# Attention scores of a hybrid encoder block: high times high as 64-row matmuls, for two query blocks in opposite halves of the array

## The chip, the cores and the metric

The kernel runs on one core of a Trainium2 chip. The metric is the device time of one execution in microseconds (us), lower is better. The engines are called as the profile calls them: PE (TensorE, the matmuls), PEld (its weight loads), DVE (VectorE), ACT (ScalarE), POOL (GpSimd), SP (SyncE, which here issues DMAs).

## What is computed

One layer of a bidirectional encoder, 1024 tokens of width 1024, all in float32. The part that matters here is the attention: two kinds, eight heads of 64 features each. Neighbourhood attention ("na") has its own keys for every head; sliding-window attention ("sw") has two key heads for eight query heads. Queries and keys are normalized by their root mean square and multiplied by gains.

```python
def rms_norm(x, g):
    xf = x.astype(jnp.float32)
    y = xf * lax.rsqrt(jnp.mean(xf * xf, axis=-1, keepdims=True) + RMS_EPS)
    return y.astype(x.dtype) * g
...
        q_a = rms_norm(q_a.reshape(B, T, NA_HEADS, HEAD_DIM), q_norm_a[l])
        k_a = rms_norm(k_a.reshape(B, T, NA_HEADS, HEAD_DIM), k_norm_a[l])
        o_a = neighbourhood_attention(q_a, k_a, v_a, rpb_a[l]).reshape(B, T, A_W)
        q_b = rms_norm(q_b.reshape(B, T, SW_HEADS, HEAD_DIM), q_norm_b[l])
        k_b = rms_norm(k_b.reshape(B, T, SW_KV_HEADS, HEAD_DIM), k_norm_b[l])
        o_b = sliding_window_attention(q_b, k_b, v_b, sink_b[l], t5_table).reshape(B, T, B_QW)
        y = (jax.nn.sigmoid(g_a) * jnp.einsum('bte,ed->btd', o_a, w_branch_a[l])
             + jax.nn.sigmoid(g_b) * jnp.einsum('bte,ed->btd', o_b, w_branch_b[l]))
        x = x + jnp.einsum('btd,de->bte', y, w_out[l])
        h = rms_norm(x, norm_ffn[l])
        u = jax.nn.silu(jnp.einsum('btd,df->btf', h, w_gate[l])) * jnp.einsum('btd,df->btf', h, w_up[l])
        x = x + jnp.einsum('btf,fd->btd', u, w_down[l])
```

Both attentions compute, for a block of queries, softmax(q k / 8 + bias) v over the keys near it.

## The kernel before

Matmuls run in a reduced float32 format ("fp32r"). To keep the precision, every operand is split in two parts: the high part is the value rounded to fp32r, the low part what is left. A product then takes three matmuls: high times high, high times low, low times high.

The tokens are permuted so that both attentions become banded: the 1024 tokens are eight blocks of 128, and a block of queries needs the keys of its own block and of the neighbours, 384 columns, or 256 for the first and the last block. The heads come in six groups (`order`, L186): four of "na" with two heads, two of "sw" with four. For every group `projection` (L236) multiplies the normalized input with the group's weights tile by tile (L325 to L327), `finish` (L329) takes the root mean squares, and `layout` (L263) transposes four tiles of queries at a time into a bank `tq` (L299) and of keys into a bank `tk` (L306).

Since a head has 64 features and the array 128 rows, a head's high and low parts share one tile. `rev_put` (L266) puts the high part of a head's queries (ACT, L277) into one half of the partitions of its tile `q`, `own`, and the low part (DVE, L278) into the other, `oth`, with the gain g multiplied in. `put_both` (L291) does the same with the keys, in a tile `k1`, and two DMAs copy it into `k2` with the halves swapped (L312, L313). The scores of a block (`scores`, L583) are then two matmuls of 128 rows into one PSUM bank: L591 with `k1` gives high times high plus low times low, L592 with `k2` the two mixed products.

The softmax follows at once: DVE adds the bias and takes the maximum (L597), ACT takes the exponential and its sum (L603), DVE the reciprocal (L604), POOL the product (L605); the result is the tile `E`, in five buffers. `flip` (L608) transposes three pieces of E on PE (L615) into a bank `tp` and splits them into `ph` (ACT, L50) and `pl` (DVE, L51); `values` (L637) multiplies these with v (L649).

The main loop (L714) goes over the 128 steps (16 heads by 8 query blocks): at step g it issues the scores of g, then the values of step g − 5, then the flip of step g − 3, and in between matmuls of the next group's projection (`fill`, L660), whose number `plan` (L712) sets. The order on PE is that of the program; the order on DVE, ACT and POOL is made by a scheduler when the kernel is built. There are two PSUM banks for scores (`s`), two for `tp`, three for projections and `tq`, `tk`, one for the output. After the attention, branch products, output projection and feed-forward (a seven-product scheme, L824 to L826) run until the end.

A table for the "sw" bias is made once near the start by a matmul with 32 rows and 8 columns (`window_table`, L542).

Of the kernel before, what the change touches and what calls it, by code (L numbers as in the profile page):

```python
# [19 lines left out]
HD = 64  # L20
# [5 lines left out]
def block_kernel(ctx, tc, x, xt, small, w_in, rpb, t5, w_ba, w_bb, w_out, w_gate, w_up, w_down,  # L26
# [18 lines left out]
    def f(ap):  # L45
        return ap.bitcast(F32)
# [55 lines left out]
    def tok(t):  # L102
        return slice(t * P, (t + 1) * P)
# [60 lines left out]
    def load_small():  # L164
        nc.scalar.dma_start(cols, small)
        nc.vector.tensor_scalar_mul(nsink, nsink, -1.0)
        for b in "ab":
            nc.vector.tensor_scalar_mul(gk[b], gk[b], HD ** 0.5)

    warm = cst.tile([P, 1], F32, name="warm")  # L170
    nc.scalar.activation(warm, mhalf[:, 0:1], AF.Exp)
# [64 lines left out]
    def projection(gi, weights, pending, after=None):  # L236
# [17 lines left out]
        def both(parts):  # L254

            if gi:
                for part in parts:
                    part()()
            else:
                for low in [part() for part in parts]:  # L260
                    low()

        def layout(s0):  # L263
            sw = kind == "sw"

            def rev_put(z, own, oth, src, g):  # L266

                if sw:
                    def to(z, rows):
                        return z[rows, :].rearrange("p (b r h x) -> p b r h x", b=8, r=2, h=2)[:, :, :, 1 - s0 // 4, :]  # L270
                    src = src.rearrange("p (b r x) -> p b r x", b=8, r=2)[:, :, ::-1, ::-1]
                else:
                    def to(z, rows):
                        return z[rows, s0 * P:(s0 + 4) * P].rearrange("p (b x) -> p b x", b=4)
                    src = src.rearrange("p (b x) -> p b x", b=4)[:, :, ::-1]
                hi_of, lo_of = to(z, own), to(z, oth)
                nc.scalar.activation(hi_of, src, AF.Copy, scale=g)  # L277
                return lambda: nc.vector.scalar_tensor_tensor(lo_of, src, g, f(hi_of), op0=ALU.mult, op1=ALU.subtract)  # L278

            def spot(tp, rows, j):  # L280
                return tp[rows, :].rearrange("p (r s c) -> p s r c", s=4, r=16)[:, j] if sw else tp[rows, tok(j)]

            def rows16(z):
                return z.rearrange("p (r x) -> p r x", r=16) if sw else z

            def put(z, rows):
                if not sw:
                    return z[rows, s0 * P:(s0 + 4) * P]
                return z[rows, :].rearrange("p (r h x) -> p r h x", r=16, h=2)[:, :, s0 // 4, :]

            def put_both(z, own, oth, src, g):  # L291
                nc.scalar.activation(put(z, own), rows16(src), AF.Copy, scale=g)
                return lambda: nc.vector.scalar_tensor_tensor(put(z, oth), rows16(src), g, f(put(z, own)),
                                                              op0=ALU.mult, op1=ALU.subtract)

            def pair(p_):
                tq = bank("pj" if gi or not s0 else "t", f"tq{gi}_{s0}_{p_}")
                for j in range(4):
                    nc.tensor.transpose(spot(tq, slice(0, P), j), qns[s0 + j][:, tok(p_)], ident)  # L299
                both([lambda e=e, own=own, oth=oth: rev_put(q[2 * p_ + e], own, oth, tq[own, :], gq[b][own, :])  # L300
                      for e, (own, oth) in enumerate(SIDES)])

            def keys():
                tk = bank("pj" if gi else "o", f"tk{gi}_{s0}")
                for j in range(4):
                    nc.tensor.transpose(spot(tk, slice(0, nk * HD), j), qns[s0 + j][:, nq * HD:nqk], ident)  # L306
                both([lambda e=e, own=own, oth=oth: put_both(k1[e], own, oth, tk[own, :], gk[b][own, :])
                      for e, (own, oth) in enumerate(SIDES[:nk])])
                for e, (own, oth) in enumerate(SIDES[:nk]):
                    for c in ([slice(0, T)] if s0 and kind == "sw" else  # L310
                              [slice(s0 * P, s0 * P + 512)] if kind == "na" else []):
                        nc.sync.dma_start(f(k2[e][oth, c]), f(k1[e][own, c]))  # L312
                        nc.sync.dma_start(f(k2[e][own, c]), f(k1[e][oth, c]))  # L313

            def done():
                if s0 == 4:
                    if late_v:
                        split(v[0][:, :, 0, :], v[0][:, :, 1, :], late_v.pop())
                    ready.add(gi)

            return [keys] + [lambda p_=p_: pair(p_) for p_ in range(nq // 2)] + [done]
# [7 lines left out]
        def finish(tiles):  # L329
# [2 lines left out]
            ss = ap.tile([P, 16], F32, tag="ss", name=f"ss{gi}_{t0}", bufs=4)[:, :n * nh]  # L332
            norms = ss.rearrange("p (t h) -> p t h", h=nh)
            for i, (t, ps) in enumerate(tiles):
                qn = ap.tile([P, 320], F32, tag="qn", name=f"qn{gi}_{t}", bufs=7)
                nc.scalar.activation(qn[:, :nqk], ps[:, :nqk], AF.Square)
                nc.vector.tensor_reduce(norms[:, i], qn[:, :nqk].rearrange("p (h e) -> p h e", e=HD),
                                        axis=AX.X, op=ALU.add)
                qns.append(qn)
# [189 lines left out]
    with tc.tile_pool(name="at", bufs=1) as ap:  # L529
# [50 lines left out]
            heads += [dict(gi=gi, kind=kind, hl=hl, kl=hl * nk // nq, h=idx * nq + hl, nq=nq, O={}, E={}, P={})  # L580
                      for hl in range(nq)]

        def scores(hd, qb):  # L583
            q, k1, k2, v = groups[hd["gi"]]
            nm_ = f"{hd['gi']}_{hd['hl']}_{qb}"
            b0, b1 = max(0, qb - 1), min(7, qb + 1)
            n = (b1 - b0 + 1) * P
            s = bank("s", "s" + nm_)
            qs = q[hd["hl"]][:, tok(qb)]
            ks = slice(b0 * P, b0 * P + n)  # L590
            nc.tensor.matmul(s[:, :n], qs, k1[hd["kl"]][:, ks], start=True, stop=False)  # L591
            nc.tensor.matmul(s[:, :n], qs, k2[hd["kl"]][:, ks], start=False, stop=True)  # L592
            E = ap.tile([P, 388], F32, tag="E", name="E" + nm_, bufs=5)
            nm = ap.tile([P, 2], F32, tag="nm", name="nm" + nm_, bufs=5)
            sw = hd["kind"] == "sw"
            sk = nsink[:, hd["h"]:hd["h"] + 1]
            att["bound"] = nc.vector.tensor_tensor_reduce(E[:, :n], s[:, :n], hd["bias"](qb), -1.0, sk if sw else 1e30,  # L597
                                           ALU.add, ALU.min, nm[:, 0:1]).ins
            m = n
            if sw:  # L600
                nc.gpsimd.tensor_copy(E[:, n:n + 1], sk)
                m = n + 1
            nc.scalar.activation(E[:, :m], E[:, :m], AF.Exp, bias=nm[:, 0:1], scale=-1.0, accum_out=nm[:, 1:2])  # L603
            nc.vector.reciprocal(nm[:, 1:2], nm[:, 1:2])  # L604
            nc.gpsimd.tensor_scalar(E[:, :n], E[:, :n], nm[:, 1:2], 1.0, op0=ALU.mult, op1=ALU.mult)  # L605
            hd["E"][qb] = E

# [106 lines left out]
        for g in range(n + LP):  # L714
            before = plan[g - 1] if g else due[0]
            if g < n:
# [2 lines left out]
                    fill(done_chunks[1] + 1)  # L719
                if g == 0:  # L720
                    opening.close()
                scores(hd, qb)
                if qb == 1 and g + 8 < n:
                    load_bias(steps[g + 8][0])
                if qb == (4 if g + 16 >= n else 6) and g + 8 - qb < n:
# [794 lines left out]
```

## Time and profile before

| what | value |
|---|---|
| median of 3 runs | 1317.51 us (1315.83 to 1317.52) |
| span of the profiled execution | 1314.8 us (no other time is given for it) |
| granted clock | 1.000 |
| busy in 54 to 120 us | PE 65.42, DVE 49.57, ACT 45.31, POOL 37.30 of 66 us |
| busy in 340 to 380 us | PE 38.74, DVE 30.76, ACT 26.18, POOL 13.43 of 40 us |
| busy in 400 to 700 us | PE 299.15, DVE 242.96, ACT 145.32 of 300 us |

The profile is of one execution. Busy times are unions of an engine's instructions; matmuls are pipelined, and their recorded durations overlap, so the distance between two starts says more of a matmul's price than its duration. A row of the timeline has the start, the time, the engine, the line, the operation, output and inputs, the shape, how many rows are merged, and in brackets the idle time before it with what ended it. "issue" there is a wait for nothing that the profile shows. For a matmul "128*128 128x384" is the loaded part (rows times columns) and what streams through it.

### The profile page before, as it was taken

The page shows a single profiled execution, that of the slowest core. Times are in us where ns is not written, and L with a number is a line of the kernel's source. Part 1 is how long each engine was busy: PE and PEld are TensorE (multiplying, and loading weights), DVE is VectorE, ACT ScalarE, POOL GpSimd, SP SyncE. Part 2 cuts the span into 40 slices and gives each one's busy share as a digit, 9 for nine tenths or more (in the row PEclk, how much of TensorE's full clock was granted, in tenths as well). Part 3 has the DMA queues.
Part 4 walks back from the last instruction along what each step waited for, and adds up shares of the span by engine and source line. Part 5 has one row for each costly group of instructions (what it writes and reads, how often), then busy time and mean ns, then how long its engine had stood idle before and what let it go on. Part 6 is the DMA issues. An engine that isn't in the chain of part 4 may idle for free.

```text
span 1314.8 us, 19624 instructions
## 1 busy us (share of the span) xinstructions
PE 1304.5 (99%) x6618; PEld 1133.6 (86%) x6618; DVE 1018.5 (77%) x2039; ACT 695.8 (53%) x1459; POOL 182.5 (14%) x322
## 2 busy tenths in 40 slices
PE   9999999999999999999999999999999999999998
PEld 8999999999888788888888888888888888888887
DVE  5678867776687758868999878888777799798774
ACT  6677857776664324636456544443444455363532
POOL 1364645564310000000000000000000000000000
PEclk9999999999999999999999999999999999999999
DMA  9532424252435348757774533233233356672532
GB/s 306 153 89 61 108 64 109 61 135 61 143 118 180 121 146 271 240 172 237 241 247 120 169 105 106 87 104 117 81 108 121 120 171 217 245 248 65 183 129 81
DMA packets 180997, 191.92 MB, mean 146 GB/s; under 512 B 21104, under 2 KB 126576, under 8 KB 180896
## 3 DMA queue, kind: packets, MB, share of 16 engines
q1 hardware_dynamic: 180640, 190.57, 46.5%
q8 instruction: 52, 0.85, 0.3%
q14 instruction: 49, 0.40, 0.1%
q10 hardware_dynamic: 256, 0.10, 0.0%
HBM read 133.19 MB, written 52.37 MB: 141 GB/s over the span
## 4 chain that ended last, share of the span: by engine, by line
PE 85%; DVE 6%; DMA 4%; ACT 2%; issue 1%; SPq 1%; POOL 1%; ACTq 0%; POOLq 0%; DVEq 0%
PE bankZ L824 6%; PE bankZ L825 5%; PE bankZ L826 5%; PE bankY L824 5%; PE bankY L826 5%; PE bankY L825 5%; PE pj L327 4%; PE bankX L824 4%; PE pj L326 4%; PE pj L325 4%; PE bankX L825 4%; PE bankX L826 4%; PE o L649 3%; PE bankV L825 3%; PE bankV L824 3%; PE bankV L826 3%
## 5 line engine op out<-in xcount | busy, mean ns | idle before, releaser
L603 ACT ACTIVATE E<-E,nm 128x384 f32<-128x384 f32 (+3 forms) x128 | 75.7, 592 | 48.3 <-DVE nm L597 42.4
L605 POOL TENSOR_SCALAR E<-E,nm 128x384 f32<-128x384 f32 (+1 forms) x128 | 74.3, 581 | 95.2 <-DVE nm L604 72.3
L51 DVE TENSOR_TENSOR pl<-tp,ph 128x384 fp32r<-128x384 f32 (+1 forms) x128 | 66.4, 519 | 17.2 <-ACT ph L50 16.2
L50 ACT CAST ph<-tp 128x384 fp32r<-128x384 f32 (+1 forms) x128 | 57.4, 449 | 20.5 <-PE tp L615 19.9
L50 ACT CAST f<-f 128x512 fp32r<-128x512 f32 x87 | 50.9, 620 | 22.2 <-DMA f<-u_dram 21.5
L51 DVE TENSOR_TENSOR f<-f 128x512 fp32r<-128x512 f32 x87 | 56.4, 684 | 8.0 <-ACT f L50 8.0
L615 PE MATMUL tp<-ident,E 128*128 128x128 f32 x352 | 59.5, 272 | 0.9 <-POOL E L605 0.9
L615 PEld LDWEIGHTS tp<-ident,E 128*128 128x128 f32 x352 | 45.2, 140 | 5.9 <-POOL E L605 1.2
L345 POOL TENSOR_TENSOR ss<-ss,mhalf 128x4 f32<-128x4 f32 (+2 forms) x42 | 49.7, 1184 | 3.2
L649 PE MATMUL o<-pl,v 128*128 128x256 f32 (+2 forms) x160 | 48.7, 305 | 0.6 <-DVE pl L51 0.5
L604 DVE RECIPROCAL nm<-nm 128x1 f32<-128x1 f32 x128 | 20.4, 160 | 36.1 <-ACT E L603 34.8
L1214 POOL TENSOR_TENSOR rs<-rs,mhalf 128x4 f32<-128x4 f32 x2 | 2.8, 1418 | 319.4 <-DVE rs L1213 319.4
L649 PE MATMUL o<-ph,v 128*128 128x256 f32 (+2 forms) x160 | 45.9, 301 | 0.5 <-ACT ph L50 0.5
L591 PE MATMUL s<-k,q 128*128 128x384 f32 (+1 forms) x128 | 46.0, 359 | 0.0
L592 PE MATMUL s<-k,q 128*128 128x384 f32 (+1 forms) x128 | 41.4, 323 | 0.0
L597 DVE CUSTOM_DVE_ANT_0 E<-s,bsw,cols 128x384 f32<-128x384 f32 (+1 forms) x64 | 37.0, 577 | 4.5 <-PE s L592 3.8
L1231 ACT ACTIVATE u<-u 128x512 f32<-128x512 f32 x44 | 27.5, 629 | 19.7 <-DVE u L1230 19.7
L597 DVE CUSTOM_DVE_ANT_0 E<-s,bna 128x384 f32<-128x384 f32 (+1 forms) x64 | 32.9, 517 | 4.2 <-PE s L592 3.7
L1232 DVE TENSOR_TENSOR u<-u,wide_rs 128x512 f32<-128x512 f32 x44 | 30.0, 687 | 6.4 <-ACT u L1231 5.6
L50 ACT CAST f_5h<-s1f 128x512 fp32r<-128x512 f32 x22 | 13.7, 622 | 39.5 <-DVE s1f L806 32.2
L824 PE MATMUL bankY<-f,f_6h 128*128 128x512 f32 x88 | 34.5, 392 | 0.1
L825 PE MATMUL bankV<-f,f_5h 128*128 128x512 f32 x88 | 34.4, 391 | 0.0
(1268 smaller groups left out, 4658.9 us busy)
## 6 DMA issues: line engine op xcount, KB each, us to landing
f<-u_dram SPq DMA_DIRECT2D x77, 256.0 KB
wg_s<-in_w_gate_dram SPq DMA_DIRECT2D x22, 512.0 KB
u_dram<-u SPq DMA_DIRECT2D x33, 256.0 KB
o_dram<-of SPq DMA_DIRECT2D x32, 256.0 KB
o<-o_dram SPq DMA_DIRECT2D x32, 256.0 KB
sg<-g_dram SPq DMA_DIRECT2D x32, 256.0 KB
g_dram<-go SPq DMA_DIRECT2D x24, 256.0 KB
u_dram<-tau SPq DMA_DIRECT2D x22, 256.0 KB
```

The source lines that it names most:

```text
L50: a = nc.scalar.copy(hi, src)
L51: b = (eng or nc.vector).tensor_tensor(lo, src, f(hi), ALU.subtract)
L325: nc.tensor.matmul(ps[:, :384], lh, his[k][:, :384], start=(k == 0), stop=False)
L326: nc.tensor.matmul(ps[:, :384], lh, los[k][:, :384], start=False, stop=False)
L597: att["bound"] = nc.vector.tensor_tensor_reduce(E[:, :n], s[:, :n], hd["bias"](qb), -1.0, sk if sw else 1e30, ALU.add, ALU.min, nm[:, 0:1] ...
L603: nc.scalar.activation(E[:, :m], E[:, :m], AF.Exp, bias=nm[:, 0:1], scale=-1.0, accum_out=nm[:, 1:2])
L605: nc.gpsimd.tensor_scalar(E[:, :n], E[:, :n], nm[:, 1:2], 1.0, op0=ALU.mult, op1=ALU.mult)
L615: nc.tensor.transpose(tp[:, tok(j)], hd["E"][qq][:, ko:ko + P], ident)
L649: nc.tensor.matmul(hd["O"][half][:, (a - half * 4) * P:(z + 1 - half * 4) * P], v[:, kb].rearrange("p a e -> p (a e)"), pp[:, (a - q0) * P ...
L824: nc.tensor.matmul(ps, hi[:, tok(j)], bh, start=first, stop=False, skip_group_check=True)
L825: nc.tensor.matmul(ps, hi[:, tok(j)], bl, start=False, stop=False, skip_group_check=True)
L826: nc.tensor.matmul(ps, lo[:, tok(j)], bh, start=False, stop=end, skip_group_check=True)
```

## The change

Each pair of query blocks (2i, 2i + 1) of a head is now scored together, on every even step. For each of the two blocks one full matmul of 128 rows gives the two mixed products; then a matmul of 64 rows gives high times high alone, for one block in the lower half of the array and for the other in the upper half (`tile_position`). For the second block's high part to lie in the other half, `rev_put` now swaps the halves for every second block, so it puts each half in two pieces. The product of the two low parts is no longer added. The queries' gain is multiplied into the keys' gain at the start. Buffers of E go from five to six, of `qn` from seven to six.

```diff
         for b in "ab":
-            nc.vector.tensor_scalar_mul(gk[b], gk[b], HD ** 0.5)
+            nc.vector.scalar_tensor_tensor(gk[b], gk[b], HD ** 0.5, gq[b], op0=ALU.mult, op1=ALU.mult)
...
-            def rev_put(z, own, oth, src, g):
+            def rev_put(z, own, oth, src):
...
-                hi_of, lo_of = to(z, own), to(z, oth)
-                nc.scalar.activation(hi_of, src, AF.Copy, scale=g)
-                return lambda: nc.vector.scalar_tensor_tensor(lo_of, src, g, f(hi_of), op0=ALU.mult, op1=ALU.subtract)
+                def part(par):
+                    own_, oth_ = (oth, own) if par else (own, oth)
+                    hi_of, lo_of = (to(z, rows)[:, par::2] for rows in (own_, oth_))
+                    nc.scalar.copy(hi_of, src[:, par::2])
+                    return lambda: nc.vector.tensor_tensor(lo_of, src[:, par::2], f(hi_of), ALU.subtract)
+
+                lows = [part(par) for par in range(2)]
+                return lambda: [low() for low in lows]
...
-                both([lambda e=e, own=own, oth=oth: rev_put(q[2 * p_ + e], own, oth, tq[own, :], gq[b][own, :])
+                both([lambda e=e, own=own, oth=oth: rev_put(q[2 * p_ + e], own, oth, tq[own, :])
...
-                qn = ap.tile([P, 320], F32, tag="qn", name=f"qn{gi}_{t}", bufs=7)
+                qn = ap.tile([P, 320], F32, tag="qn", name=f"qn{gi}_{t}", bufs=6)
...
-        def scores(hd, qb):
+        def scores(hd, qa):
+
             q, k1, k2, v = groups[hd["gi"]]
+            z, kl = q[hd["hl"]], hd["kl"]
+            high = [k1[kl], k2[kl]] if kl == 0 else [k2[kl], k1[kl]]
+            made = []
+            for par in range(2):
+                qb, e = qa + par, (hd["hl"] + par) % 2
+                b0, b1 = max(0, qb - 1), min(7, qb + 1)
+                n, ks = (b1 - b0 + 1) * P, slice(b0 * P, (b1 + 1) * P)
+                s = bank("s", f"s{hd['gi']}_{hd['hl']}_{qb}")
+                made.append((qb, e, s, n, ks))
+                nc.tensor.matmul(s[:, :n], z[:, tok(qb)], high[1 - e][:, ks], start=True, stop=False)
+            for qb, e, s, n, ks in made:
+                rows = slice(e * HD, (e + 1) * HD)
+                nc.tensor.matmul(s[:, :n], z[rows, tok(qb)], high[e][rows, ks], start=False, stop=True,
+                                 tile_position=(e * HD, 0))
+            for qb, e, s, n, ks in made:
+                softmax(hd, qb, s, n)
+
+        def softmax(hd, qb, s, n):
+
             nm_ = f"{hd['gi']}_{hd['hl']}_{qb}"
-            b0, b1 = max(0, qb - 1), min(7, qb + 1)
-            n = (b1 - b0 + 1) * P
-            s = bank("s", "s" + nm_)
-            qs = q[hd["hl"]][:, tok(qb)]
-            ks = slice(b0 * P, b0 * P + n)
-            nc.tensor.matmul(s[:, :n], qs, k1[hd["kl"]][:, ks], start=True, stop=False)
-            nc.tensor.matmul(s[:, :n], qs, k2[hd["kl"]][:, ks], start=False, stop=True)
-            E = ap.tile([P, 388], F32, tag="E", name="E" + nm_, bufs=5)
-            nm = ap.tile([P, 2], F32, tag="nm", name="nm" + nm_, bufs=5)
+            E = ap.tile([P, 388], F32, tag="E", name="E" + nm_, bufs=6)
+            nm = ap.tile([P, 2], F32, tag="nm", name="nm" + nm_, bufs=6)
...
-                scores(hd, qb)
+                if not qb % 2:
+                    scores(hd, qb)
```

In the changed kernel the full score matmuls are L600 and the 64-row ones L603; the first operation of the softmax is L615 there, the transposes of `flip` L633, the values L667, the projections L330 to L332.

On PE, in the second group's last head, the rows around block 2 before the change. The names are the output and then the inputs: `s_3_2` is the score bank of head 3 of the group, block 2, `tp` the flipped bank, `pj` the projection's:

```order
L615 MATMUL tp_2_6_2291<-ident,E_2_6_2161 128x128
L615 MATMUL tp_2_6_2291<-ident,E_2_7_2198 128x128
L591 MATMUL s_3_2_2299<-k_0_655,q_3_653 128x384
L592 MATMUL s_3_2_2299<-k_0_656,q_3_653 128x384
L325 MATMUL pj_0_2227<-wg_5h,h_0_94 128x384
L326 MATMUL pj_0_2227<-wg_5l,h_0_94 128x384
L327 MATMUL pj_0_2227<-wg_5h,h_0_94 128x384
```

Block 3 follows eighteen rows after block 2, behind the next flip:

```order
L615 MATMUL tp_2_7_2335<-ident,E_2_6_2161 128x128
L615 MATMUL tp_2_7_2335<-ident,E_2_7_2198 128x128
L591 MATMUL s_3_3_2342<-k_0_655,q_3_653 128x384
L592 MATMUL s_3_3_2342<-k_0_656,q_3_653 128x384
L325 MATMUL pj_0_2227<-wg_7h,h_0_95 128x384
```

The same place of PE after the change:

```order
L633 MATMUL tp_2_6_2319<-ident,E_2_6_2192 128x128
L633 MATMUL tp_2_6_2319<-ident,E_2_7_2199 128x128
L600 MATMUL s_3_2_2327<-k_0_659,q_3_657 128x384
L600 MATMUL s_3_3_2329<-k_0_660,q_3_657 128x384
L603 MATMUL s_3_2_2327<-k_0_660,q_3_657 128x384
L603 MATMUL s_3_3_2329<-k_0_659,q_3_657 128x384
L330 MATMUL pj_0_2255<-wg_5h,h_0_94 128x384
L331 MATMUL pj_0_2255<-wg_5l,h_0_94 128x384
L332 MATMUL pj_0_2255<-wg_5h,h_0_94 128x384
```

The two score matmuls of block 3 have moved up beside those of block 2, into one run of four, of which the two L603 have 64 rows.

On DVE, the same two blocks before (`E` is the softmax tile, `pl` the low part of a flipped one, `nm` the maximum and the sum; the L597 row named ISA is the bias and the maximum):

```order
L597 ISA E_3_2_2302,nm_3_2_2303<-s_3_2_2299,bsw_1989,cols 128x384
L597 ISA nm_3_2_2303 128x1
L51 TENSOR_TENSOR pl_2_6_2296<-tp_2_6_2291,ph_2_6_2295 128x384
L604 RECIPROCAL nm_3_2_2303<-nm_3_2_2303 128x1
L597 ISA E_3_3_2345,nm_3_3_2346<-s_3_3_2342,bsw_1989,cols 128x384
L597 ISA nm_3_3_2346 128x1
L293 SCALAR_TENSOR_TENSOR k_0_1197<-tk_4_2322,cols,k_0_1197 64x512
```

And after the change:

```order
L615 ISA E_3_2_2333,nm_3_2_2334<-s_3_2_2327,bsw_2017,cols 128x384
L615 ISA nm_3_2_2334 128x1
L51 TENSOR_TENSOR pl_2_6_2324<-tp_2_6_2319,ph_2_6_2323 128x384
L615 ISA E_3_3_2340,nm_3_3_2341<-s_3_3_2329,bsw_2017,cols 128x384
L615 ISA nm_3_3_2341 128x1
L622 RECIPROCAL nm_3_2_2334<-nm_3_2_2334 128x1
L622 RECIPROCAL nm_3_3_2341<-nm_3_3_2341 128x1
L298 SCALAR_TENSOR_TENSOR k_0_1213<-tk_4_2360,cols,k_0_1213 64x512
```

The second block's bias and maximum stand ahead of the first block's reciprocal now, and both reciprocals follow together.

On DVE again, where the queries of the second group are laid out, before (`tq` is the bank of transposed queries, `q` the tile of a head):

```order
L278 SCALAR_TENSOR_TENSOR q_0_650<-tq_0_0_931,cols,q_0_650 64x16x32
L51 TENSOR_TENSOR pl_0_1_948<-tp_0_1_943,ph_0_1_947 128x384
L597 ISA E_0_5_957,nm_0_5_958<-s_0_5_954,bna_294 128x384
L597 ISA nm_0_5_958 128x1
L278 SCALAR_TENSOR_TENSOR q_1_651<-tq_0_0_931,cols,q_1_651 64x16x32
```

And after:

```order
L622 RECIPROCAL nm_0_5_937<-nm_0_5_937 128x1
L280 TENSOR_TENSOR q_0_654<-tq_0_0_948,q_0_654 64x4x2x32 x2
L51 TENSOR_TENSOR pl_0_1_969<-tp_0_1_964,ph_0_1_968 128x384
L280 TENSOR_TENSOR q_1_655<-tq_0_0_948,q_1_655 64x4x2x32 x2
L342 TENSOR_REDUCE ss_5_981<-qn_5_982 128x5
```

Each put of a query's low part is two instructions ("x2") of half the columns in place of one.

## The prediction

> **What bounds the kernel now.** I read the page first (busy shares, then the chain that ended last), then the waits of TensorE in the attention stage, the busy times by stretch, and last the timeline around single matmuls.
>
> ```profile
> span 1314.8 us, 19624 instructions
> ...
> PE 1304.5 (99%) x6618; PEld 1133.6 (86%) x6618; DVE 1018.5 (77%) x2039; ACT 695.8 (53%) x1459; POOL 182.5 (14%) x322
> ...
> PE 85%; DVE 6%; DMA 4%; ACT 2%; issue 1%; SPq 1%; POOL 1%; ACTq 0%; POOLq 0%; DVEq 0%
> ```
>
> PE is busy for 99% of the span and carries 85% of the chain. The score matmuls, which the change touches, stand in one stage:
>
> ```profile
> L591 PE MATMUL s<-k,q x128: 278/341/423, 55.7 to 380.0; 128*128 128x384 f32 x96, 128*128 128x256 f32 x32
> ```
>
> So 128 score tiles (96 of 384 columns, 32 of 256) are made between 55.7 and 380.0 us, one every 2.55 us. In that stage PE waits for other engines only this long (engine, line, releaser: total us, times, longest):
>
> ```profile
> PE tp L615 <- POOL E L605: 0.9, 1, 0.9
> PE tq L299 <- DVE k L293: 0.6, 1, 0.6
> PE o L649 <- DVE pl L51: 0.5, 2, 0.3
> PE o L649 <- ACT ph L50: 0.5, 1, 0.5
> PE tk L306 <- DVE qn L366: 0.5, 1, 0.5
> PE pj L326 <- DVE wg_6l L51: 0.2, 1, 0.2
> ```
>
> That is 3.2 us in all, of 324. A PE time added or saved there moves the end one for one, except for what these 3.2 us can take up. The other engines have room; the next row has a stretch, its length, the busy time (and instructions) of PE, PEld, DVE, ACT and POOL, then the granted clock and the DMA:
>
> ```profile
> 212.00:265.00 53.00, 52.90 (x350) 51.67 (x349) 41.81 (x135) 39.95 (x110) 25.75 (x58) 1.00 0.31 80
> ```
>
> DVE, the fullest of them, has 41.81 of 53 us, 79%.
>
> **The price of a matmul.** A matmul's duration in the records overlaps the next one's, so I go by the distance between starts.
>
> ```profile
> 302.25 0.34 PE L327 MATMUL pj<-wg_7h,h 128*128 128x384 f32 x1
> 302.43 0.33 PE L591 MATMUL s<-k,q 128*128 128x384 f32 x1
> 302.60 0.33 PE L592 MATMUL s<-k,q 128*128 128x384 f32 x1
> 302.78 0.33 PE L325 MATMUL pj<-wg_0h,h 128*128 128x384 f32 x1
> ...
> 306.84 0.28 PE L649 MATMUL o<-ph,v 128*128 128x256 f32 x1
> 306.96 0.28 PE L649 MATMUL o<-pl,v 128*128 128x256 f32 x1
> 307.08 0.34 PE L325 MATMUL pj<-wg_6h,h 128*128 128x384 f32 x1
> ...
> 307.62 0.60 PE L306 MATMUL tk<-ident,qn 128*128 128x128 f32 x4
> 308.05 0.49 PE L615 MATMUL tp<-ident,E 128*128 128x128 f32 x3
> ```
>
> 384 columns take 0.175 us (0.35 for the two from 302.43 to 302.78), 256 columns 0.12, and 128 columns in plain float32 0.108 (four in 0.43, so 512 such columns 0.43). The weight loads hide behind the matmul before.
>
> **What changes on PE.** Per pair of query blocks there were four full matmuls, two to a block; now there are two full ones and two of 64 rows, in the lower and the upper half. If the halves ran wholly side by side and nothing else cost anything, one matmul of 0.175 would go per inner pair. But the program now goes from 128 rows to 64 and back in each of 64 pairs, and the trace has one place where the row shape changes: the table product L542, of 32 rows and 8 columns, between full matmuls. First PE, then its weight loads:
>
> ```profile
> 24.29 0.33 PE L326 MATMUL pj<-wg_7l,h 128*128 128x384 f32 x1
> 24.46 0.34 PE L327 MATMUL pj<-wg_7h,h 128*128 128x384 f32 x1
> 24.73 1.02 PE L542 MATMUL pswe<-oh,t5s 32*8 32x512 f32 x2
> 25.68 0.44 PE L325 MATMUL pj<-wg_0h,h 128*128 128x384 f32 x1
> 25.96 0.33 PE L326 MATMUL pj<-wg_0l,h 128*128 128x384 f32 x1
> ```
>
> ```profile
> 24.29 0.19 PEld L327 LDWEIGHTS pj<-wg_7h,h 128*128 128x128 f32 x1
> 24.73 0.09 PEld L542 LDWEIGHTS pswe<-oh,t5s 32*8 32x8 f32 x2 [0.25 <-issue]
> 25.68 0.19 PEld L325 LDWEIGHTS pj<-wg_0h,h 128*128 128x128 f32 x1 [0.86 <-ACT rows L150]
> 25.79 0.19 PEld L326 LDWEIGHTS pj<-wg_0l,h 128*128 128x128 f32 x1
> ```
>
> Everywhere else a load starts with the matmul before it (24.29 and 24.29). Here the load of L542 does not start at 24.46 but at 24.73, and "issue" says that it waited for nothing the profile shows. **Going in** costs 0.27 − 0.175 = 0.095. **Coming out**: two passes of 0.43 from 24.73 end at 25.59, and the next load starts at 25.68, 0.09 later; that load then lies bare, since the matmul behind it starts 0.28 after it, not 0.175, which is 0.105 more. The row names ACT's L150 as releaser; what L325 takes from ACT there is a part of h, written before the rows of x are squared, so I take the gap for the shape's. Going in, the load of L542 has only 8 columns; a score's has 128, so I add a bare load of 0.105 there too. Two changes of shape: 0.095 + 0.105 + 0.09 + 0.105 = 0.395 us per pair.
>
> The second half needs a load as well. The nearest row has the next load 0.11 after a bare one (25.68, 25.79), so I start the second half 0.11 after the first; side by side with it, this is 0 (both loads at once), one behind the other 0.175. Then:
> - two inner pairs per head (384 and 384): the halves took 2 × 0.175 = 0.35; now 0.395 + 0.11 + 0.175 = 0.68; +0.33 each.
> - first pair (256, 384): 0.295 before; 0.68 now; +0.385.
> - last pair (384, 256): 0.295 before; 0.395 + 0.11 + 0.12 = 0.625 now; +0.33.
> Per head 0.33 × 3 + 0.385 = 1.375, for 16 heads **+22.0 us**. With both loads at once it is 0.22 × 2 + 0.275 × 2 = 0.99, +15.8; with the halves one behind the other 4 × 0.395, +25.3. I take the row's 0.11 and keep both ends.
>
> A change of columns alone shows no such price:
>
> ```profile
> 92.28 0.33 PE L327 MATMUL pj<-wg_6h,h 128*128 128x384 f32 x1
> 92.46 0.60 PE L306 MATMUL tk<-ident,qn 128*64 128x128 f32 x4
> ```
>
> The transposes with 64 columns follow at the usual 0.18. The Trainium skill, "TensorEngine Tiling (Array Packing)", section Key Properties, says that changing the tiling mode drains the TensorE, and makes no difference between rows and columns. The row shape at 24.73 agrees with its 0.095, the column shape at 92.46 does not; by the rule the sum stays at +22.0, without it it would be the first rival's.
>
> **What else changes.** The queries' parts are now put in two pieces each: 32 puts become 64, on ACT and on DVE.
>
> ```profile
> L277 ACT ACTIVATE q<-tq,cols x32: 667/685/688, 39.4 to 344.1; 64x512 fp32r<-64x512 f32 x32
> ...
> L278 DVE SCALAR_TENSOR_TENSOR q<-tq,cols,q x32: 744/750/758, 40.8 to 344.8; 64x512 fp32r<-64x512 f32 x32
> ...
> L50 ACT CAST ph<-tp 128x256 fp32r<-128x256 f32 x31 | 11.4, 368 | 8.7 <-PE tp L615 8.3
> ...
> L51 DVE TENSOR_TENSOR pl<-tp,ph 128x256 fp32r<-128x256 f32 x31 | 13.0, 419 | 5.4 <-ACT ph L50 4.8
> ```
>
> A piece of 256 columns costs 0.368 on ACT and 0.419 on DVE by the nearest rows, so 32 × (0.736 − 0.685) = 1.6 us more of ACT and 32 × (0.838 − 0.750) = 2.8 us of DVE. PE's own work hides them; uncovered they cost up to 4.4. The gains that leave L277 and L278 go into the key gain, one instruction in place of one at the start: nothing. The softmaxes now come two at a time:
>
> ```profile
> L603 ACT ACTIVATE E<-E,nm 128x384 f32<-128x384 f32 (+3 forms) x128 | 75.7, 592 | 48.3 <-DVE nm L597 42.4
> L605 POOL TENSOR_SCALAR E<-E,nm 128x384 f32<-128x384 f32 (+1 forms) x128 | 74.3, 581 | 95.2 <-DVE nm L604 72.3
> ...
> L604 DVE RECIPROCAL nm<-nm 128x1 f32<-128x1 f32 x128 | 20.4, 160 | 36.1 <-ACT E L603 34.8
> ...
> L597 DVE CUSTOM_DVE_ANT_0 E<-s,bsw,cols 128x384 f32<-128x384 f32 (+1 forms) x64 | 37.0, 577 | 4.5 <-PE s L592 3.8
> ```
>
> One takes 0.577 + 0.592 + 0.16 + 0.581 = 1.9 us, the second some 0.6 more; the flip that needs it stands two steps on, 5.1 us, so PE's other work covers it. Behind the second L597 on DVE stand both reciprocals, then the next flip's low part, which the values need two steps later: covered too. If that cover were gone in the few places where PE waits already, those 3.2 us might double; the odd block's E being made a step earlier may take away the 0.9 behind POOL's E. Six E buffers where there were five keep the distance to reuse; one qn buffer less could show as a longer wait of tq or tk (0.6 and 0.5 now). I take 0 for all of this, with −1 to +4.
>
> Against it, PE falls behind by 1.375 us per head, and each present wait is under 1 us, so the other engines catch up: I take off all 3.2 us (ends 0 and 3.2).
>
> **Sum.** 22.0 − 3.2 = +18.8 us on a span of 1314.8: 1333.6. No separate time is given for the profiled execution; its span lies 2.7 under the median of the three timed runs, 1317.5, so the forecast is 1317.5 + 18.8 = **1336.3 us**, 1.4% slower.
>
> **Rivals.**
> - *No price for the shape* (the one that ends faster): loads stay hidden, the halves overlap. Inner pair 0.175 + 0.11 against 0.35, −0.065; first −0.01; last −0.065: −0.205 per head, −3.3 us, 1314.2. With both loads at once −0.175 and −0.12, twice each: −9.4 us, 1308.1. For it: the 64-column transposes, and that L542 is one place, of another size. Against: nothing else explains 24.73. It decides if the two changes together cost under 0.065 to 0.175 us per pair.
> - *Both loads at once*: the halves start together, +15.8 − 3.2 = +12.6, 1330.1. The Trainium skill, "TensorE: Matmul & The Clock Gate", section "Part 3: Packing small matmuls — row/col tiling", has matmuls of different row groups start about 4 ns apart, and loads overlap running matmuls only where the row group differs; no row here shows two row groups at work. For it: the two loads of L542 stand within 0.09 us; against: these have 8 columns.
> - *Halves not side by side*: the change then does not do what it says. With the price +25.3 − 3.2 = +22.1, 1339.6; without it no change, 1317.5.
> - *Only one way costs* (say coming out): 0.1975 per pair, the halves overlapping: 0.1325 × 3 + 0.1875 per head, +9.4, less half of the 3.2: +7.8, 1325.3.
>
> **How the numbers follow.** Forecast 0.38, both loads at once 0.20, one behind the other with the price 0.08, one way only 0.06: slower 0.72. No price with overlap 0.17, half of it at −9.4 and half at −3.3; no change at all 0.11. A measurement of this kernel tells about 0.2%, 2.6 us, from no change; part of the −3.3 falls inside that, so faster 0.14, same 0.14. The likeliest case's own range, with the side terms, is 1329 to 1343. The 8-in-10 range leaves out the no-price cases (0.17) and little else: **1316 to 1343**.
>
> **What would show it.** In the changed trace: the load of the first half (L603) starts with its matmul some 0.27 after the second full one (L600) rather than beside it, and the next full matmul's load starts about 0.09 after the halves' end with the following matmul 0.28 on; from the first full matmul of a pair to the one after it I expect about 1.03 us, where it was 0.70. Only L600 and L603 and their neighbours should be farther apart; after 400 us everything should be shifted, not longer. I am wrong if the loads of L603 start beside the matmuls ahead of them, or if the waits behind DVE and POOL grow past 5 us.

## The result and the profile after

| | before | after |
|---|---|---|
| median, range | 1317.51 us (1315.83 to 1317.78, 4 runs) | 1336.51 us (1335.52 to 1337.96, 4 runs) |
| profiled execution, span | 1314.8 us | 1335.4 us (its time 1337.23) |

The ratio is 1.0153, with an interval of 1.0139 to 1.0167: 19.0 us slower, where 18.8 were forecast. The total was right, but by luck: terms of it were wrong, and their errors cancelled. The three lines of the page that answer to those of before:

```profile
span 1335.4 us, 19668 instructions
...
PE 1321.6 (99%) x6618; PEld 1124.0 (84%) x6618; DVE 1024.9 (77%) x2071; ACT 695.3 (52%) x1491; POOL 182.1 (14%) x322
...
PE 86%; DVE 4%; DMA 4%; POOL 2%; ACT 1%; issue 1%; SPq 1%; ACTq 0%; POOLq 0%; DVEq 0%
```

PE is still the bound, with as many matmuls as before. The end of the program is only shifted. One matmul of the feed-forward, from the view of its tile, first in the kernel before, then in the one after (first and last start at the end):

```profile
L826 PE MATMUL bankV<-f,f_5l x88: 389/389/389, 686.7 to 1073.4; 128*128 128x512 f32 x88
```

```profile
L845 PE MATMUL bankV<-f,f_5l x88: 389/389/389, 707.5 to 1093.9; 128*128 128x512 f32 x88
```

It starts 20.8 us later at its first instance and 20.5 later at its last, so all of the time came ahead of it. One inner pair of the kernel after, from the timeline, PE and then its weight loads (two rows merged are "x2", the time then runs from the first start to the last end):

```profile
227.24 0.51 PE L600 MATMUL s<-k,q 128*128 128x384 f32 x2
227.69 0.44 PE L603 MATMUL s<-k,q 64*128 64x384 f32 x2
228.06 0.44 PE L330 MATMUL pj<-wg_2h,h 128*128 128x384 f32 x1
228.34 0.34 PE L331 MATMUL pj<-wg_2l,h 128*128 128x384 f32 x1
```

```profile
227.08 0.36 PEld L600 LDWEIGHTS s<-k,q 128*128 128x128 f32 x2
227.69 0.19 PEld L603 LDWEIGHTS s<-k,q 64*128 64x128 f32 x2 [0.25 <-issue]
228.06 0.19 PEld L330 LDWEIGHTS pj<-wg_2h,h 128*128 128x128 f32 x1 [0.19 <-issue]
```

From the first full matmul to the halves 0.45 us, from the halves to the next full matmul 0.37, from that to its successor 0.28: 1.10 us, where five full matmuls in a row need 5 × 0.175 = 0.875. That is +0.225 for this pair. The load of the halves waits for "issue", as L542's did, and it does so in all 64 pairs, 14.4 us together. The two loads of L603 together last 0.19, as long as one, and its two matmuls 0.44, as long as a single matmul behind a bare load (L330 at 228.06): the halves start together. For a pair of 384 and 256 columns:

```profile
204.26 0.47 PE L600 MATMUL s<-k,q 128*128 128x384 f32 x2
204.65 0.44 PE L603 MATMUL s<-k,q 64*128 64x384 f32 x2
205.02 0.44 PE L330 MATMUL pj<-wg_7h,h 128*128 128x384 f32 x1
205.30 0.34 PE L331 MATMUL pj<-wg_7l,h 128*128 128x384 f32 x1
```

This is 1.04 us against 2 × (0.175 + 0.12) + 0.175 = 0.765, +0.275. With two pairs of each kind per head that is 16 × 2 × (0.22 + 0.275), the prediction's +15.8 us for both loads at once. What PE waited for in the attention stage (50 to 410 us; total us, times, longest):

```profile
PE o L667 <- DVE pl L51: 3.3, 5, 0.9
PE o L667 <- ACT ph L50: 1.3, 2, 0.8
PE tk L311 <- DVE nm L622: 0.5, 1, 0.5
PE tq L304 <- DVE k L298: 0.4, 1, 0.4
PE tq L304 <- DVE q L280: 0.2, 1, 0.2
```

These waits were 3.2 us before and are 5.7 now; the new ones are in front of `values`, for `ph` and `pl`. Just after the worst of them the clock falls. Two stretches, with the busy times of PE, PEld, DVE, ACT and POOL, then the granted clock:

```profile
157.00:166.00 9.00, 7.15 (x43) 6.20 (x43) 5.55 (x19) 5.91 (x18) 5.85 (x11) 0.99 0.66 189
166.00:169.50 3.50, 3.50 (x13) 2.75 (x12) 1.70 (x6) 1.82 (x5) 0.92 (x3) 0.53 0.23 62
```

After 9 us in which PE was idle for 1.85, the clock was 0.53 for 3.5 us, which costs about 3.5 × 0.47 = 1.6 us. The Trainium skill, "TensorE: Matmul & The Clock Gate", section "What's actually happening", has the clock halve after an idle window of some 3.4 us; the halving agrees, but no single wait of PE in the list above is longer than 0.9 us. What sets the halving off is not shown: the 9 us from 287 us on have 1.70 us of idle PE, and the 3.5 us behind them a clock of 1.00; and of the four executions one had a mean clock of 1.000 (1335.52 us).

### The profile page after: what moved, and what is told of

It reads as the page before. It is cut to its first block, busy times and chain, and to the rows that moved or that the text cites. A ratio compares the mean times of both kernels' runs of the same rounds, so it can differ in the third digit from the quotient of the medians.

```text
span 1335.4 us, 19668 instructions
## 1 busy us (share of the span) xinstructions
PE 1321.6 (99%) x6618; PEld 1124.0 (84%) x6618; DVE 1024.9 (77%) x2071; ACT 695.3 (52%) x1491; POOL 182.1 (14%) x322
## 4 chain that ended last, share of the span: by engine, by line
PE 86%; DVE 4%; DMA 4%; POOL 2%; ACT 1%; issue 1%; SPq 1%; ACTq 0%; POOLq 0%; DVEq 0%
PE bankZ L843 6%; PE bankZ L844 6%; PE bankZ L845 6%; PE bankY L844 5%; PE bankY L843 5%; PE bankY L845 5%; PE pj L330 5%; PE bankX L843 4%; PE bankX L845 4%; PE bankX L844 4%; PE pj L332 4%; PE pj L331 4%; PE o L667 3%; PE bankV L844 3%; PE bankV L843 3%; PE bankV L845 3%
## 5 line engine op out<-in xcount | busy, mean ns | idle before, releaser
L633 PE MATMUL tp<-ident,E 128*128 128x128 f32 x352 | 59.3, 272 | 0.0
L667 PE MATMUL o<-pl,v 128*128 128x256 f32 (+2 forms) x160 | 49.2, 308 | 3.3 <-DVE pl L51 3.3
L633 PEld LDWEIGHTS tp<-ident,E 128*128 128x128 f32 x352 | 45.1, 140 | 4.7
L667 PE MATMUL o<-ph,v 128*128 128x256 f32 (+2 forms) x160 | 46.8, 306 | 1.3 <-ACT ph L50 1.3
L615 DVE CUSTOM_DVE_ANT_0 E<-s,bsw,cols 128x384 f32<-128x384 f32 (+1 forms) x64 | 35.3, 580 | 9.4 <-PE s L603 7.6
L615 DVE CUSTOM_DVE_ANT_0 E<-s,bna 128x384 f32<-128x384 f32 (+1 forms) x64 | 31.2, 521 | 9.0 <-PE s L603 7.3
L667 PEld LDWEIGHTS o<-pl,v 128*128 128x128 f32 x160 | 30.6, 191 | 5.4 <-DVE pl L51 4.4
L843 PE MATMUL bankZ<-f,f_4h 128*128 128x512 f32 x88 | 34.5, 392 | 0.4 <-DVE p L1367 0.4
L844 PE MATMUL bankV<-f,f_5h 128*128 128x512 f32 x88 | 34.4, 391 | 0.0
L843 PE MATMUL bankV<-f,f_5h 128*128 128x512 f32 x88 | 34.4, 391 | 0.0
L844 PE MATMUL bankZ<-f,f_4h 128*128 128x512 f32 x88 | 34.4, 390 | 0.0
```

The costliest lines, as they stand in the source:

```text
L633: nc.tensor.transpose(tp[:, tok(j)], hd["E"][qq][:, ko:ko + P], ident)
L667: nc.tensor.matmul(hd["O"][half][:, (a - half * 4) * P:(z + 1 - half * 4) * P], v[:, kb].rearrange("p a e -> p (a e)"), pp[:, (a - q0) * P ...
L843: nc.tensor.matmul(ps, hi[:, tok(j)], bh, start=first, stop=False, skip_group_check=True)
L844: nc.tensor.matmul(ps, hi[:, tok(j)], bl, start=False, stop=False, skip_group_check=True)
```

## The experiments

The theory after the first look: the price of the row shape is that of both loads at once, +15.8 us, and pairing the scores adds waits. The rivals: the halves don't overlap, the two-piece puts cost something, or the pairing costs nothing and the shape all.

**Pairing with full rows.** L603 again with all 128 rows, which adds the product of the low parts; all else as after.

```diff
-                rows = slice(e * HD, (e + 1) * HD)
-                nc.tensor.matmul(s[:, :n], z[rows, tok(qb)], high[e][rows, ks], start=False, stop=True,
-                                 tile_position=(e * HD, 0))
+                nc.tensor.matmul(s[:, :n], z[:, tok(qb)], high[e][:, ks], start=False, stop=True)
```

> The changed kernel with the second two matmuls of a pair at 128 rows again (which adds the product of the low parts back); pairing, swapped halves, two-piece puts and buffers stay. Shape theory: the changes of row shape cost 0.22 us a pair as the starts in the changed trace show, 15.8 us in all, so 1336.5 - 15.8 = 1320.7 us, 1319 to 1323. Rival, pairing: the time comes from softmaxes two at a time and from the puts, and it stays above 1330.

Measured 1327.60 us (1322.55 to 1329.13), ratio 1.0071 (1.0048 to 1.0094). A miss for both theories: without any change of shape the pairing already costs about 10 us. Much of that goes with the clock: the one of the four executions whose mean clock was 1.000 took 1322.55 us, 5.4 over the median of the kernel before at 1.000 in the same runs (1317.15), and the other three (0.997 to 0.999) 1326.53 and more. In the profiled execution, at 0.999, in 50 to 410 us PE waits 3.7 us for `pl`, 1.6 for `ph`, 1.6 for a transfer of the keys and 2.3 for smaller ones, 9.2 in all, and the clock falls here too:

```profile
163.00:165.00 2.00, 2.00 (x9) 2.00 (x8) 1.13 (x4) 0.89 (x2) 0.45 (x2) 0.51 0.44 120
165.00:168.00 3.00, 3.00 (x19) 2.96 (x18) 0.74 (x4) 1.42 (x5) 0.85 (x3) 0.76 0.03 5
```

**A half alone.** The kernel before, block by block, with its second score matmul over 64 rows; the product of the low parts is left out.

```diff
-            nc.tensor.matmul(s[:, :n], qs, k1[hd["kl"]][:, ks], start=True, stop=False)
-            nc.tensor.matmul(s[:, :n], qs, k2[hd["kl"]][:, ks], start=False, stop=True)
+            nc.tensor.matmul(s[:, :n], qs, high[1 - e][:, ks], start=True, stop=False)
+            nc.tensor.matmul(s[:, :n], z[rows, tok(qb)], high[e][rows, ks], start=False, stop=True,
+                             tile_position=(e * HD, 0))
```

> The kernel before, unpaired, with the mixed products at 128 rows and high times high at 64 rows, one half alone per block (the product of the low parts is left out). Shape theory: 128 blocks pay going in and coming out with nothing side by side, 0.39 us each, +50 us: 1367, 1362 to 1372. Rival, the pair's 0.37 us from the first half to the next full matmul is two loads one behind the other and no wait after the halves: 0.29 each, +37 us: 1354.

Measured 1362.06 us (1360.54 to 1363.80), ratio 1.0340 (1.0324 to 1.0355): the price comes with every change of shape, so twice as often. One block and then the waits of PE in 50 to 410 us:

```profile
209.57 0.34 PE L594 MATMUL s<-k,q 128*128 128x384 f32 x1
209.84 0.44 PE L595 MATMUL s<-k,q 64*128 64x384 f32 x1
210.21 0.44 PE L325 MATMUL pj<-wg_3h,h 128*128 128x384 f32 x1
```

```profile
PE tq L299 <- DVE k L293: 0.2, 1, 0.2
```

Going in takes 0.27 and from the half to the next full matmul 0.37, the same 0.37 as with two halves: the second half is free. Of 3.2 us of waits 0.2 are left, so here PE's delay did take them up. 128 × 0.395 − 3.0 is +47.6; the span grew by 46.4, of which 44.3 stand ahead of the feed-forward (its first bankV starts at 731.0, before at 686.7) and about 1.7 are a stretch from 745.2 to 748.6 us at a clock of 0.51. So the sum is some 3 us high; that was not attributed.

**Both in one half.** The kernel after with both blocks in the same half of the array.

```diff
-                    own_, oth_ = (oth, own) if par else (own, oth)
+                    own_, oth_ = own, oth
...
-                qb, e = qa + par, (hd["hl"] + par) % 2
+                qb, e = qa + par, hd["hl"] % 2
```

> The changed kernel with both blocks' high parts in the same half of the array, no swap. If the halves run side by side in the changed kernel, this loses it: 0.175 for two inner pairs and 0.12 for two outer pairs of a head, 9.4 us on top of 1336.5: 1346, more (1351) if the second half's load lies bare too. Rival, they do not overlap now: 1336.5 as it is.

Measured 1344.01 us (1341.77 to 1345.83), ratio 1.0197 (1.0179 to 1.0214), 7.5 us over the kernel after. The pair that stood at 227.24:

```profile
228.84 0.51 PE L600 MATMUL s<-k,q 128*128 128x384 f32 x2
229.28 0.61 PE L603 MATMUL s<-k,q 64*128 64x384 f32 x2
229.83 0.45 PE L330 MATMUL pj<-wg_2h,h 128*128 128x384 f32 x1
```

The halves now take 0.55 instead of 0.37: one streams after the other. So in the kernel after they do lie side by side. The loss of 7.5 is less than the 9.4 expected; this trace has no stretch of half clock (1.6 us in the kernel after).

**The two-piece puts alone.** The kernel before with each half put in two pieces (not swapped), the gain in the keys and six `qn` buffers.

> The kernel before with the queries put in two pieces (not swapped), the gain moved to the keys and six qn buffers; scores as before. Shape theory: hidden, 1317.5 within 2.6. Rival, puts: some 4 us slower, 1321.

Measured 1316.46 us (1314.70 to 1319.14, 10 runs), ratio 0.9994 (0.9985 to 1.0003): no difference, as taken in the prediction.

**What pairing waits for.** The waits of the kernel after for `ph` and `pl` lead to the weights of the next group, whose last two pieces are split into parts (`wg_6h`, `wg_7h` on ACT, `wg_6l` on DVE) from a staging tile `wg_3s`. ACT, then PE, then DVE in the kernel after:

```profile
162.11 0.51 ACT L50 CAST wg_6h<-wg_3s 128x384 fp32r<-128x384 f32 x1 [2.42 <-DMA wg_3s<-in_w_in_dram]
162.53 0.51 ACT L50 CAST wg_7h<-wg_3s 128x384 fp32r<-128x384 f32 x1
162.94 0.47 ACT L50 CAST ph<-tp 128x384 fp32r<-128x384 f32 x1
```

```profile
162.35 0.34 PE L332 MATMUL pj<-wg_3h,h 128*128 128x384 f32 x1
163.47 0.33 PE L667 MATMUL o<-ph,v 128*128 128x128 f32 x1 [0.77 <-ACT ph L50]
164.68 0.33 PE L667 MATMUL o<-pl,v 128*128 128x128 f32 x1 [0.89 <-DVE pl L51]
```

```profile
162.66 0.56 DVE L51 TENSOR_TENSOR wg_6l<-wg_3s,wg_6h 128x384 fp32r<-128x384 f32 x1 [2.36 <-ACT wg_6h L50]
163.13 0.48 DVE L615 CUSTOM_DVE_ANT_0 E<-s,bsw,cols 128x256 f32<-128x256 f32 x1
...
163.53 0.61 DVE L615 CUSTOM_DVE_ANT_0 E<-s,bsw,cols 128x384 f32<-128x384 f32 x1
...
164.07 0.55 DVE L51 TENSOR_TENSOR pl<-tp,ph 128x384 fp32r<-128x384 f32 x1
```

A wait in brackets counts from the recorded end of the matmul before it. L332 and L667 start 1.12 us apart where 0.175 is usual, so the listed 0.77 costs 0.95: a wait behind such a matmul costs some 0.17 us more than the lists say. ACT stands for 2.42 us behind a transfer, with `ph` behind it on the same engine; DVE stands behind ACT and then works through two score blocks before `pl`. The same splits on ACT in the kernel before:

```profile
154.31 0.49 ACT L50 CAST ph<-tp 128x384 fp32r<-128x384 f32 x1
154.78 0.51 ACT L50 CAST wg_6h<-wg_3s 128x384 fp32r<-128x384 f32 x1
...
275.09 0.51 ACT L50 CAST wg_6h<-wg_3s 128x384 fp32r<-128x384 f32 x1 [0.52 <-DMA wg_3s<-in_w_in_dram]
...
275.92 0.47 ACT L50 CAST ph<-tp 128x384 fp32r<-128x384 f32 x1
```

There one `ph` stood ahead of the split, and the other behind it, for a transfer that was 0.52 us late; in the kernel after both stand behind it, and both transfers are some 2.4 us late. The view of the tile `wg_3s` sums such waits of ACT, before and then after:

```profile
  DMA wg_3s<-in_w_in_dram: 0.7, 2
```

```profile
  DMA wg_3s<-in_w_in_dram: 5.2, 3
```

The theory became: the pairing's cost is this split ahead of `ph`. The rival: it is the two softmaxes that now come at once. Four runs, with the two splits issued later, in the first tile of the next group's projection:

```diff
-                if after and t == 7 and k:
+                if gi > 1 and t == 0 and k in (1, 3):
+                    weights.split(6 + k // 2)
+                if after and t == 7 and 0 < k < 7:
                     after.split(k - 1)
...
-            if after and t == 7:
-                after.split(7)
```

on the kernel after,

> The changed kernel with the splits of the last two weight tiles of a group (which on ACT wait for the transfer of wg_3s, with a flip's ph queued behind them) moved behind the start of the next group. If the time beside the shape's 15.8 us comes from there, the stalls near 163 and 293 us of the changed trace go, with the half clock that follows the first: some 6 us, 1330.5, 1329 to 1333. If it comes from elsewhere: 1336.5.

on the pairing with full rows,

> The paired kernel with full rows (e1_full_rows) and the same late splits. Wait theory: from 1327.6 to 1321, 1319 to 1323. Rival, two softmaxes at a time: 1327.6 stays.

on the kernel before,

> The kernel before with the late splits alone. It has one such stall, of 1.1 us near 276 us: 1316.5, within 0.2% of before under every theory; a control, and perhaps the fastest.

and, without the later splits, the pairing with full rows with the odd block's softmax at its own step:

```diff
-            for qb, e, s, n, ks in made:
-                softmax(hd, qb, s, n)
+            (qb, e, s, n, ks), (qb1, e1, s1, n1, ks1) = made
+            softmax(hd, qb, s, n)
+            att["odd"] = lambda: softmax(hd, qb1, s1, n1)
...
                 if not qb % 2:
                     scores(hd, qb)
+                else:
+                    att["odd"]()
```

> e1_full_rows with the odd block's softmax issued at its own step, so that only the matmuls are paired. If pairing costs by two softmaxes at a time on DVE, ACT and POOL: back to 1317.7, within 2.6. If it costs by the weights' wait or by where the matmuls stand: 1325 or more.

Measured: 1334.68 us (ratio 1.0133, 1.0111 to 1.0154), 1323.38 (1.0048, 1.0029 to 1.0066), 1317.99 (1.0007, 0.9997 to 1.0017) and 1325.08 (1.0063, 1.0038 to 1.0088). By the medians the first gained only 1.8 of the 6 us expected (2.6 by the ratios to the kernel before of the same runs): the scheduler put the split ahead of `ph` again.

```profile
161.10 0.51 ACT L50 CAST wg_6h<-wg_3s 128x384 fp32r<-128x384 f32 x1 [1.72 <-DMA wg_3s<-in_w_in_dram]
161.52 0.47 ACT L50 CAST ph<-tp 128x384 fp32r<-128x384 f32 x1
```

The second came to 1323.38, between the 1321 and the 1327.6 expected, and still waits 5.0 us in three splits. So these runs decided nothing on the split, except that the kernel before is indifferent to it. The fourth speaks against the rival: 1325.08 lies inside the range of 1322.55 to 1329.13 that the full-row pairing has without it, though DVE's order kept two score blocks ahead of `pl`, so the rival was not fully taken away.

**The splits fixed behind `ph`.** The two splits at k of 3 and 4, now with an order that the scheduler must keep: behind the last `ph` on ACT and the last bound of the attention.

```diff
+                if gi > 1 and t == 0 and k in (3, 4):
+                    with tc.issue_after(att["ph"]), tc.issue_after(att["bound"]):
+                        weights.split(3 + k)
...
-            _, att["bound"] = split(*(z[:, :n].rearrange("p (j i) -> p j i", i=P) for z in (ph, pl)),
+            att["ph"], att["bound"] = split(*(z[:, :n].rearrange("p (j i) -> p j i", i=P) for z in (ph, pl)),
```

On the pairing with full rows,

> e6_full_rows_late again, with the two late splits ordered on ACT behind the last flip's ph (in e6 the order on ACT had not changed: wg_6h still stood ahead of ph_2_4). Wait theory: the waits of the values for ph and pl near 163 and 286 us, 4.4 us with their bare loads, go, and it comes to 1319, 1317 to 1321. Rival, the pairing costs by itself: 1323 stays.

on the kernel after,

> The changed kernel with the same order. What is left is then the shape's price: 0.22 for inner and 0.27 for outer pairs, 15.8 us over before, 1333, 1331 to 1334.5. If the shape costs less than the starts say, it is below 1330; if the pairing costs beside it, above 1335.

on the kernel before,

> The kernel before with the same order: its one such stall, 1.1 us near 276 us, goes: 1316.4, within 0.2% of before. A control.

and on the two-piece puts alone:

> e4_puts_alone with the same order; the puts measured nothing, so as the control: 1316, a fastest version if any of these is.

Measured, beside 1317.83 us for the kernel before in the same runs:

| kernel | median | ratio (interval) |
|---|---|---|
| full rows, splits behind | 1319.71 us | 1.0022 (1.0011 to 1.0033) |
| after, splits behind | 1331.37 | 1.0110 (1.0092 to 1.0127) |
| before, splits behind | 1315.09 | 0.9985 (0.9972 to 0.9997) |
| puts alone, splits behind | 1315.79 | 0.9987 (0.9973 to 1.0001) |

Both paired kernels got faster, by 7.9 and 5.1 us (6.5 and 5.7 by the ratios, each to the kernel before of its own runs), and into the ranges expected. ACT of the kernel after with the splits behind, then the waits of PE in 50 to 410 us, and the stretch whose clock was 0.53:

```profile
162.98 0.48 ACT L50 CAST ph<-tp 128x384 fp32r<-128x384 f32 x1
...
163.96 0.50 ACT L50 CAST wg_6h<-wg_3s 128x384 fp32r<-128x384 f32 x1
```

```profile
PE o L668 <- DVE pl L51: 1.5, 3, 0.6
PE tk L311 <- DVE nm L623: 0.5, 1, 0.5
PE tq L304 <- DVE k L298: 0.4, 1, 0.4
PE pj L331 <- DVE wg_6l L51: 0.4, 1, 0.4
PE tq L304 <- DVE q L280: 0.2, 1, 0.2
```

```profile
166.00:169.50 3.50, 3.50 (x25) 3.43 (x25) 2.14 (x7) 3.03 (x9) 1.76 (x6) 1.00 0.29 78
```

This `wg_6h` no longer waits for its transfer, no wait for `ph` is left, and the clock stays at 1.00. The waits are 3.0 us, about as many as before the change, so what is left of the change in this trace is the shape: the span is 1330.3 us, 15.5 over the kernel before, and the price of the pairs with both loads at once is 15.8. The times say a little less, though the interval reaches over all of this: 13.5 us by the medians, 14.5 by the ratio (12.1 to 16.7), and 14.9 among executions at a mean clock of 1.000 (all four here, 14 of 25 of the kernel before). Of the full-row pairing 1.9 us remain by the medians, 0.2%, at the edge of what a measurement of this kernel can tell. Its trace has no wait for `ph` left either, but 5.6 us of waits in all, 1.7 of them for a transfer of the keys. Since it still has two softmaxes at once, the rival has at most these few us. No kernel beats the one before by more than can be told: the best, with the splits behind, lies within 0.2%, and the interval reaches to 0.9997.

## Why the prediction was right, and where it was not

- **PE is the bound, and what is added there moves the end**: right. The feed-forward is shifted by 20.5 to 20.8 us and no longer than it was.
- **Going in, 0.095**: right. 0.45 from the first full matmul to the halves is 0.175 + 0.275, the 0.27 of L542, though L542 has 32 rows and 8 columns. The Trainium skill, "TensorEngine Tiling (Array Packing)", section Key Properties, has a change of tiling mode drain the TensorE: the trace agrees for the change of row shape, in the pairs shown here as in L542.
- **Coming out, 0.09, and two bare loads of 0.105**: right. From the start of the halves 0.105 + 0.175 lead to 227.97, and the next load starts at 228.06; 0.28 on from there comes the next matmul. That everywhere else a load starts with the matmul before it is too much said: behind the float32 transposes a load lies partly bare too, in the kernel before as well (L325 at 304.83, L326 0.25 later). The 0.09 ahead of the load is what the change of shape alone showed.
- **The second half 0.11 after the first**: this step failed. It was taken from the distance between two loads of full height; two loads in opposite halves run together, and 0.37 us pass whether one half or two are at work (the half alone, the same half). The term is +15.8, not +22.0: 6.2 too much. The span of the kernel with the splits behind agrees, 15.5 with about the waits of before. It was the rival "both loads at once" that got the price right; the Trainium skill's 4 ns between matmuls of different row groups ("TensorE: Matmul & The Clock Gate", section "Part 3: Packing small matmuls — row/col tiling"), named there, fits rows that agree to 0.01 us.
- **All 3.2 us of waits taken up**: this step failed too. It holds for the unpaired half, where 0.2 us are left. But the paired kernel waits 5.7 us, and 3.0 with the splits behind.
- **Side terms 0, from −1 to +4**: too low. The puts and the `qn` buffer are hidden, as was said (the sixth E buffer was not tried alone). But the prediction costed the pairing by how long two softmaxes take and who waits for them; it did not look at what stands ahead of `ph` on ACT. There the split of the weights waits for its transfer, 5.2 us where it was 0.7, and at 162.11 it has moved ahead of a `ph` that it stood behind. In the kernel after that is 2.5 us more of waits and 1.6 of half clock; fixing the order gave back 5.1 us.
- **The sum**: 15.8 + 2.5 + 1.6 = 19.9 us, of 20.6 in the spans; of the other 0.7 some 0.5 may be the 0.17 us that a wait costs beyond its listed time, for ten waits where there were seven. What was too much for the second half (6.2) was about what was too little for the waits and the clock (3.2 + 2.5 + 1.6 = 7.3): that the total came out is luck.
- **What was to show it**: the load of L603 at 0.27 and the next load 0.09 behind the halves came as said. From the first full matmul to the start of the next one I had 1.03 us with its bare load; it is 0.82 + 0.105 = 0.925. The waits behind DVE and POOL stayed under the 5 us named (4.4 behind DVE); the other 1.3 are for ACT, which the prediction had not named.
- **Rivals**: "no price" falls by every pair shown; "not side by side" by the kernel with both in one half, 7.5 us slower; "only one way" by 0.27 in and 0.09 + 0.105 out.

Open: why the transfer of `wg_3s` is late for ACT in the paired kernels. Moving the split behind `ph` cures the wait. The traces show two parts of it. Counted from SP's first issue of the transfer, ACT reaches the split after 3.45 us (162.11 − 2.42, issue at 156.24) and 3.24 us in the kernel after, and after 4.14 and 4.05 in the kernel before: some 0.7 us sooner. And the data is there after 5.9 and 5.6 us, where it took at most 4.1 and 4.6. What makes the transfer itself longer was not separated. Of the 12.5 us by which the span of the first full-row pairing grew, 6.0 are listed waits of PE in the attention, some 1.7 the clock, and 2.3 waits of PE for ACT's work on `bankZ` behind 410 us (2.7 where it was 0.4); the rest was not attributed. A version with more than two blocks to one change of shape, which would pay the 0.395 less often, was not tried.

## What to carry to other kernels

Packing two half-height matmuls side by side saves one streaming time, here 0.175 us, and pays for the way into the other row shape and back, here 0.395 us with two weight loads that nothing covers; so by these figures it could gain only where at least three such pairs stand behind one change of shape, which no run here tried. Batching work of a bound engine also moves what a scheduler places around it: look for an instruction that waits for a transfer ahead of one that the bound engine waits for, on the same engine, and fix the order there. And a forecast that hits in total says little until its terms have been measured one by one.

## What the hardware showed beyond that

- Two 64-row loads in opposite halves run at the same time (0.19 us for both), and so do the matmuls; in the same half the pair takes 0.18 us longer (0.55 against 0.37).
- The price of the row shape was the same for 64 rows with 128 columns as for 32 rows with 8: 0.27 us going in, 0.09 coming out.
- A stretch in which PE was idle for 1.85 of 9 us, no single wait over 0.9 us, was followed by 3.5 us at a clock of 0.53; the full-row pairing showed 0.51 near the same place, and with the splits behind, the clock stayed at 1.00. It isn't a rule: 1.70 of 9 us idle, later in the same execution, was followed by 1.00, and the kernel before with the splits behind, without such waits in its attention, showed 0.51 from 699.0 to 705.9 us, in the feed-forward, where PE waited 1.26 us for `bankZ`.
